# A hybrid decoder layer on one core: 32-row transposes in sample attention, one page-table transfer, ScalarE ahead of VectorE at shared PSUM banks, and larger convolution transposes

## The chip, the cores and the metric

The kernel runs on one core of one Trainium2 chip. The core has five engines with instruction streams of their own: TensorE (PE in the profile, its weight loads PEld), VectorE (DVE), ScalarE (ACT), GpSimd (POOL) and SyncE (SP, which here only issues transfers). TensorE writes to PSUM, eight banks of 128 partitions by 512 float32 values; the other engines copy from there to SBUF. The metric is the device time of one execution in microseconds. The kernel before takes 2293.38 us (median of three runs, 2289.61 to 2296.15).

## The reference

One step of a one-layer decoder trunk, all in float32: 256 prompt tokens and 8 sample sequences of 8 tokens, model width 2048. Cut to what matters here:

```
mod = silu(c) @ w_ada + b_ada                      # shift, scale, gate
h = rms_norm(x) * (1 + scale) + shift
a_qkv, a_z, a_b, a_a, b_q, b_k, b_v, b_z, i_q, i_k, i_w, g_a, g_b = split(h @ w_in)
# mixer A: short convolution (width 4, with a state of 3 old inputs), gated delta rule
qkv, conv_new = causal_short_conv(a_qkv, state_conv, conv_w)
y_a, s_new = gated_delta_rule(q, k, v, g, beta, state_gdn) -> norm, * silu(z)
# mixer B: an indexer picks the 256 best keys of each query, then attention over them
logits = einsum('bqhd,bkd->bqhk', i_q, kidx); score = sum_h relu(logits) * i_w
idx = top_k(score, 256)
y_b = softmax(q k_sel^T) v_sel * silu(b_z)
# for the samples, keys come from paged caches: kidx = cache_kidx[page_table], K, V likewise
out = x + gate * rms_norm((sigmoid(g_a) * (y_a @ w_pa) + sigmoid(g_b) * (y_b @ w_pb)) @ w_out)
```

Each sample has 1024 cached keys in 8 pages of 128. The outputs include the new delta-rule state and the last three inputs of the convolution (`conv_new`) for the prompt and for each sample.

## The kernel before

**The stream.** After a startup (`startup`, about 146 us, in which `w_ada` and the first blocks of `w_in` are read), TensorE goes through 480 units (`stream`, L342). A unit multiplies half of the 2048 rows of one 128-column block of weights with the 320 tokens: 24 matmuls of 128x320, since float32 is built from a high and a low part of weight and input (`whi`, `wlo`; `xh`, `xl`). ScalarE writes `whi` and VectorE `wlo` from the raw block, two units ahead (`split_ahead`, L326). The results go to two PSUM banks, `pm`. The order of the units is fixed: queries of the indexer, of attention, the gate of attention and gate A (units 0 to 127), then the delta-rule inputs in eight groups of two query/key heads and four value heads (units 128 to about 351; the profile calls its stage 780 to 1810 us), then gate B, the output projections and `w_out`.

**Side work.** Everything else is written as Python generators, and the order of the program is the order in which they are called: after the 12th and the 24th matmul of a unit, `side_round` (L259) lets each generator go on whose `yield` time has come by a clock of the kernel's own (`class Clock`, L68, which prices each instruction when the program is built). What a generator emits there stands on each engine's queue in that order, and every engine runs its queue in order. A generator that needs a PSUM bank takes it from the ring `ps_side` of six banks (`need`, `psum`), and gives it back when it has emitted the last reader; banks go round in turn.

**Sample attention** is one generator (`sample_branch`, L1125 on). For each of the eight samples, `keys_t` turns 8 blocks of 128x128 indexer keys (two banks of four, copied by VectorE); then come the scores (`qiS`, `wsel`), 32 rounds of top-k on VectorE, and per sample: `k_trans` (16 blocks of keys in four banks, copied by ScalarE and VectorE in turn), the products with the queries (`qS`, `esel`), the softmax, the transposes of the probabilities (8 blocks and one of 64 columns), the product with V (the last part from `vS`) and the output transpose. A transpose is a matmul with an identity matrix: the block is the loaded operand, and `ident` moves through. The keys are gathered by indices that `rows` (L753) computes from the page table, which `fetch` (L748) reads in eight transfers, each to 16 partitions.

**Convolution.** For each group, `conv_gen` (L674 on) brings old inputs (24 rows) and taps (4 rows) of 8 blocks of 128 channels to a tile `cst` of [28, 512], turns four blocks at a time (28x128 each), and VectorE copies them to `cs`. When a group's inputs are done, `ct_gen` (L1475) turns four blocks of 128x27 (`ct`) into a PSUM bank, ScalarE copies 27x512 to `cst`, and SP sends two or four transfers to the outputs.

**Delta-rule chains.** For each of 16 heads, `prompt_chain` (L1770) runs a chain of steps, each of which multiplies into one bank that both ScalarE and VectorE then read. In step 1 (names `w`, `wf`) ScalarE and VectorE take turns per value head: ScalarE scales the first 128 columns, VectorE scales the same columns, then both the next 128. Step 3 (`x1`, `ot`) and step 4 take turns likewise; `sample_chain` step 2, `bz_done` and `out_done` have VectorE first. In the program, two such readers of one bank wait for each other.

## Time and profile before

| What | Value |
|---|---|
| Median of three runs | 2293.38 us (2289.61 to 2296.15) |
| The profiled execution: its own time; its span in the trace | 2290.62 us; 2288.9 us |
| PE (matmuls) busy | 2207.7 us, 96% of the span |
| PEld (weight loads) busy | 2072.5 us, 91% |
| DVE, ACT, POOL busy | 1368.2 (60%), 1012.9 (44%), 470.6 us (21%) |
| 3 x 3328 stream matmuls of 128x320 on `w_in` | 1063.8, 1031.1 and 1029.5 us busy |
| Bytes read, written from HBM | 382.10 MB, 47.89 MB |

How to read it: every instruction is emitted through a helper, so all have line L56, and rows are told apart by the names of their tiles. `ps<-ident,a` is a transpose into a side bank of a block from the buffers `a` (keys, probabilities), `pm<-xh,whi` a stream matmul. Matmuls overlap: a row's length counts the run of one matmul through the array, so costs on TensorE are read from the starts of successive rows. Time after `[` is idle time before an instruction, with what ended it. The execution's own time is 1.7 us longer than the span.

### The profile page before, as it was taken

How to read it: one execution, taken by the hardware profiler on the slowest of the kernel's cores; microseconds unless marked ns; L12 is line 12 of the kernel's file. 1: busy time of each engine (PE TensorE's matmuls, PEld its weight loads, DVE VectorE, ACT ScalarE, POOL GpSimd, SP SyncE). 2: the span in 40 equal slices, each digit the busy share in tenths (PEclk: the TensorE clock that was granted, in tenths of full speed). 3: DMA queues.
4: the chain of work that ended last, by engine and by line, in shares of the span. 5: the costliest groups of instructions: out<-in, count | busy, mean ns of one | idle time of the engine just before them, and what ended most of it. 6: DMA issues, size and time to landing. Idle time of an engine off the chain costs nothing.

```text
span 2288.9 us, 41315 instructions
## 1 busy us (share of the span) xinstructions
PE 2207.7 (96%) x16448; PEld 2072.5 (91%) x16448; DVE 1368.2 (60%) x2666; ACT 1012.9 (44%) x2191; POOL 470.6 (21%) x624
## 2 busy tenths in 40 slices
PE   5989999999999999999999999999999999999997
PEld 3778988999988999898989898989898999999997
DVE  3333445889744567676868686868655545555433
ACT  2224355433333355554746464646454533333342
POOL 2000010000000026080818081818080000000000
PEclk9999999999999999999999999999999999999999
DMA  9989544334465557465757575756575866544543
GB/s 301 345 279 289 168 159 142 111 111 147 161 214 193 187 170 220 141 209 154 234 151 221 157 229 147 222 155 217 163 225 156 276 222 196 186 153 148 166 138 102
DMA packets 472961, 432.96 MB, mean 189 GB/s; under 512 B 63736, under 2 KB 461704, under 8 KB 470400
## 3 DMA queue, kind: packets, MB, share of 16 engines
q1 hardware_dynamic: 468384, 406.61, 57.0%
q0 software_dynamic: 3840, 21.02, 2.6%
q8 instruction: 129, 2.11, 0.4%
q10 hardware_dynamic: 544, 2.70, 0.4%
q14 instruction: 64, 0.52, 0.1%
HBM read 382.10 MB, written 47.89 MB: 188 GB/s over the span
## 4 chain that ended last, share of the span: by engine, by line
PE 77%; DVE 10%; ACT 4%; DMA 4%; POOL 2%; issue 1%; SPq 1%; DVEq 0%; POOLq 0%; ACTq 0%
PE pm L56 63%; PE ps L56 14%; DVE S L56 2%; DVE wlo L56 2%; DMA raw<-in_w_ada_dram 2%; SPq L56 1%; ACT whi L56 1%; DVE ps L56 1%; POOL X L56 1%; POOL tmpx L56 1%; ACT ot L56 1%; DVE w L56 1%; ACT ps L56 1%; DVE st L56 1%; DMA raw<-in_w_in_dram 0%
## 5 line engine op out<-in xcount | busy, mean ns | idle before, releaser
L56 PE MATMUL pm<-xh,whi 128*128 128x320 f32 x3328 | 1063.8, 320 | 2.4 <-ACT whi L56 2.4
L56 PE MATMUL pm<-xh,wlo 128*128 128x320 f32 x3328 | 1031.1, 310 | 5.8 <-DVE wlo L56 5.7
L56 PE MATMUL pm<-xl,whi 128*128 128x320 f32 x3328 | 1029.5, 309 | 0.0
L56 DVE TENSOR_TENSOR wlo<-raw,whi 128x1024 fp32r<-128x1024 f32 x480 | 600.6, 1255 | 377.4 <-ACT whi L56 376.4
L56 PEld LDWEIGHTS pm<-xh,whi 128*128 128x128 f32 x3328 | 627.2, 188 | 33.4 <-issue 25.4
L56 PEld LDWEIGHTS pm<-xh,wlo 128*128 128x128 f32 x3328 | 626.3, 188 | 8.7 <-DVE wlo L56 8.5
L56 PEld LDWEIGHTS pm<-xl,whi 128*128 128x128 f32 x3328 | 627.1, 188 | 1.0
L56 ACT ACTIVATE whi<-raw 128x1024 fp32r<-128x1024 f32 x480 | 504.4, 1056 | 262.4 <-PE pm L56 223.9
L56 POOL TENSOR_TENSOR X<-X,tmpx 48x31 f32<-48x31 f32 (+15 forms) x248 | 182.9, 738 | 19.4
L56 POOL TENSOR_TENSOR tmpx<-blk,X 48x31 f32<-48x31 f32 (+15 forms) x248 | 170.4, 687 | 44.2 <-DMA blk<-d_b 25.8
L56 PE MATMUL pm<-y1h,wlo 128*128 128x320 f32 x512 | 157.9, 308 | 0.7 <-DVE wlo L56 0.7
L56 PE MATMUL pm<-y1h,whi 128*128 128x320 f32 x512 | 157.8, 308 | 0.0
L56 PE MATMUL pm<-y1l,whi 128*128 128x320 f32 x512 | 157.8, 308 | 0.0
L56 POOL TENSOR_TENSOR sc<-sc,mh 128x6 f32<-128x6 f32 (+1 forms) x24 | 42.3, 1764 | 450.1 <-DVE sc L56 436.4
L56 DVE SCALAR_TENSOR_TENSOR ps<-xp,cs,ps 128x344 f32<-128x344 f32 x192 | 111.5, 581 | 6.8
L56 POOL TENSOR_TENSOR rfin<-rfin,mh 128x3 f32<-128x3 f32 x1 | 0.8, 848 | 495.5 <-DVE rfin L56 495.5
L56 PEld LDWEIGHTS pm<-y1h,wlo 128*128 128x128 f32 x512 | 95.9, 187 | 0.9 <-DVE wlo L56 0.9
L56 PEld LDWEIGHTS pm<-y1l,whi 128*128 128x128 f32 x512 | 96.0, 187 | 0.0
L56 PEld LDWEIGHTS pm<-y1h,whi 128*128 128x128 f32 x512 | 96.0, 187 | 0.0
L56 ACT ACTIVATE vt<-ps,sc 128x128 f32<-128x128 f32 (+1 forms) x112 | 42.5, 410 | 81.2 <-DVE w L56 64.1
L56 DVE SCALAR_TENSOR_TENSOR S<-S,gtr,ps 128x128 f32<-128x128 f32 x256 | 67.5, 343 | 1.2 <-PE ps L56 1.1
L56 ACT ACTIVATE xp<-pm 128x256 f32<-128x256 f32 (+1 forms) x128 | 31.9, 302 | 71.9 <-PE pm L56 71.7
(310 smaller groups left out, 2322.1 us busy)
## 6 DMA issues: line engine op xcount, KB each, us to landing
raw<-in_w_in_dram SPq DMA_DIRECT2D x176, 1024.0 KB
raw<-in_w_pa_dram SPq DMA_DIRECT2D x32, 1024.0 KB
rawx<-in_w_ada_dram SPq DMA_DIRECT2D x17, 1024.0 KB
a<-in_w_ada_dram SPq DMA_DIRECT2D x16, 1024.0 KB
S<-in_state_gdn_dram SPq DMA_DIRECT2D x32, 512.0 KB
out_dram<-S SPq DMA_DIRECT2D x32, 512.0 KB
raw<-in_w_pb_dram SPq DMA_DIRECT2D x16, 1024.0 KB
raw<-in_w_out_dram SPq DMA_DIRECT2D x16, 1024.0 KB
```

The source lines that it names most:

```text
L56: made = fn(*args, **kw)
```

## The change

Four things are changed.

- **Sample attention's transposes.** `tr4` splits a 128x128 transpose in four of 32 rows, each on its own 32 rows of the array and into its own bank; `out4` copies each bank, with a stride, to its place: ScalarE the even banks, VectorE the odd ones. `keys_t`, `k_trans` and the transposes of the probabilities use it. A step asks for four (or five) side banks at once where it asked for one, several times.
- **Page table.** One transfer to 8 partitions, one of 16 rows each, into a tile that VectorE has zeroed; a matmul with the matrix `samer` then spreads it to all partitions.
- **ScalarE first** where ScalarE and VectorE read one bank: `bz_done`, `prompt_chain` steps 1, 3 and 4, `sample_chain` step 2 and `out_done`. `Clock` now lets a reader of a bank start after the other engine's readers of it, and prices a 32-row transpose at 0.01.
- **Convolution.** `cst` becomes two tiles of [128, 256] that hold two channel ranges at rows 0 to 27 and 64 to 91, so that two transposes of 92x128 do what four of 28x128 did (eight input transfers a group, as before). `ct` is [128, 4, 32], zeroed at the start; one transpose of 128x128 takes the place of four of 128x27, ScalarE copies 128x128, and SP sends eight transfers for each of a group's two calls instead of four or two.

```diff
@@ class Clock @@
-                return max(outs[0].shape[-1], 32) * 2 / 2400.0
+                return 0.01 if ins[0].shape[0] == 32 else max(outs[0].shape[-1], 32) * 2 / 2400.0
...
+        if name in ("vector", "scalar"):
+            banks = {a.tensor.name for a in outs + ins if a.space == MEM.PSUM}
+            for b in banks:
+                start = max([start] + [t for e, t in self.bank.get(b, {}).items() if e != name])
@@ helpers @@
+    def tr4(self, banks, j, in_):
+        for g in range(4):
+            r = slice(32 * g, 32 * g + 32)
...
+            self.nc.tensor.transpose(banks[g][:, 32 * j:32 * j + 32], in_[r], self.ident[r, r])
+    def out4(self, banks, n, dst):
+        d = dst.rearrange("p (j g c) -> p j g c", g=4, c=32)
+        for g, p in enumerate(banks):
+            v = p[:, 0:32 * n].rearrange("p (j c) -> p j c", c=32)
+            if g % 2:
+                self.nc.vector.tensor_copy(d[:, :, g, :], v)
+            else:
+                self.act(d[:, :, g, :], v)
+            self.ps_side.put(p)
@@ conv_gen @@
-            for k in range(4):
-                self.tr(p[:, 28 * k:28 * k + 28], t[0:28, 128 * k:128 * (k + 1)])
+            for k in range(2):
+                self.tr(p[:, 128 * k:128 * k + 92], t[0:92, 128 * k:128 * (k + 1)])
@@ attn_consts: fetch, rows @@
-            for s in range(PAGES):
-                nc.gpsimd.dma_start(pt[16 * s:16 * s + 16, :],
-                                    i["page_table"][:, s:s + 1].rearrange("b o -> o b").to_broadcast([16, NB]))
+            nc.gpsimd.dma_start(pt.rearrange("(s r) b -> s r b", r=16)[:, 0, :], i["page_table"].rearrange("b s -> s b"))
...
-            nc.vector.tensor_scalar(ptf, pt, page, 16.0, op0=OP.subtract, op1=OP.mult)
+            nc.vector.tensor_copy(ptf, pt)
+            p = self.ps_main.get()
+            self.mm(p[:, 0:NB], self.samer, ptf)
+            self.ts(ptf, p[:, 0:NB], page, 16.0, OP.subtract, OP.mult)
@@ k_trans (keys_t and the probabilities alike) @@
-            for s in range(4):
-                yield from self.need(self.ps_side)
...
-                for e in range(4):
-                    self.tr(p[:, 128 * e:128 * e + 128], k[:, 128 * e:128 * e + 128])
...
+            yield from self.need(self.ps_side, 4)
+            ps = [self.psum() for _ in range(4)]
+            for j in range(16):
+                self.tr4(ps, j, K[b][:, 128 * j:128 * j + 128])
+            self.out4(ps, 16, K[b])
@@ ct_gen @@
-        for e in range(4):
-            self.tr(p[0:27, 128 * e:128 * e + 128], ct[:, e, :])
-        self.act(s, p[0:27, :])
+        self.tr(p[:, 0:128], ct.rearrange("p e r -> p (e r)"))
+        self.act(st[:, 0:128], p[:, 0:128])
...
+        for e, c0 in enumerate(cols):
+            nc.sync.dma_start(cp[:, c0:c0 + 128], st[32 * e:32 * e + 3, 0:128])
+            nc.sync.dma_start(cs[:, c0:c0 + 128], st[32 * e + 3:32 * e + 27, 0:128])
@@ prompt_chain step 1 (steps 3 and 4 alike) @@
         for v in range(2):
             self.act(wf[:, v, :], p[:, 128 * v:128 * v + 128], AF.Copy, scale=s(v, 0))
+        for v in range(2):
             self.ts(wt[:, v, :], p[:, 128 * v:128 * v + 128], stl(v, 0), None, OP.mult)
```

Since the clock prices have changed, the planner puts side work at other places of the stream. Three places follow, each first before and then after the change.

The first is TensorE's queue in the score phase of sample attention (units 45 to 46), where `a_...,qiS` are a sample's logits, `a_...,wsel` their weighted sum, and `pm` the stream. Before:

```order
L56 MATMUL ps_69<-a_1087,qiS 128x512
L56 MATMUL ps_70<-a_1087,qiS 128x512
L56 MATMUL ps_71<-kidxT,qiS 128x64
L56 MATMUL pm_66<-xh,whi_80 128x320
L56 MATMUL pm_66<-xl,whi_80 128x320
L56 MATMUL pm_66<-xh,wlo_83 128x320
```

After, a place near unit 46:

```order
L56 MATMUL ps_71<-ident,a_1086 128x32
L56 MATMUL ps_72<-a_1087,wsel 8x512 x2
L56 MATMUL ps_72<-a_1087,wsel 8x64
L56 MATMUL ps_68<-a_1086,qiS 128x512
L56 MATMUL ps_67<-a_1086,qiS 128x512
L56 MATMUL ps_69<-kidxT,qiS 128x64
L56 MATMUL ps_70<-a_1087,wsel 8x512 x2
L56 MATMUL ps_70<-a_1087,wsel 8x64
L56 LDWEIGHTS ident_b
L56 MATMUL ps_71<-bp,ident_b 128x128
```

Before, a sample's logits stand between stream matmuls, and its two `wsel` rows come 12 stream matmuls later; after, the last transposes, the weighted sums of two samples, the logits of the last and the first `ident_b` products of the next part stand in one row with no stream matmul among them.

The second is TensorE's queue at the end of sample attention, the last sample's product with V (`a,a` and `vS`). Before, in unit 121, with the output transpose `ps_72<-ident,a_1089` 23 rows further down, in unit 122:

```order
L56 MATMUL pm_66<-xh,wlo_82 128x320
L56 MATMUL ps_71<-a_1085,a_1088 64x128 x16
L56 MATMUL ps_71<-vS,a_1088 64x128 x2
L56 MATMUL pm_66<-xh,whi_79 128x320
L56 MATMUL pm_66<-xl,whi_79 128x320
L56 MATMUL pm_66<-xh,wlo_82 128x320
```

After, just ahead of unit 128, which opens the delta-rule stage:

```order
L56 MATMUL pm_66<-xl,whi_79 128x320
L56 MATMUL pm_66<-xh,wlo_82 128x320
L56 MATMUL ps_68<-a_1084,a_1087 64x128 x16
L56 MATMUL ps_68<-vS,a_1087 64x128 x2
L56 MATMUL ps_67<-ident,a_1088 128x128
L56 MATMUL pm_65<-xh,whi_80 128x320
```

The last product with V and the last output transpose moved from units 121 and 122 to the end of unit 127, behind one another, with no stream matmul between them.

The third is VectorE's queue around steps 1 and 4 of a prompt chain in the delta-rule stage, with the engines whose signals a row waits for; `w` is the result of VectorE's scaling, and ScalarE reads the same bank `ps` (for its `vt` in step 1, its `ot` in step 4). Before:

```order
L56 SCALAR_TENSOR_TENSOR S_6349<-S_6349,gtr,ps_71 128x128 x3
L56 TENSOR_TENSOR wlo_82<-raw_76,whi_79 128x1024 [waits DMAHW1_49,Activation_49]
L56 TENSOR_SCALAR w_6340<-ps_72,sc_6351 128x128 [waits DVE_49,Activation_49]
L56 TENSOR_SCALAR w_6340<-ps_72,sc_6351 128x128 [waits Activation_49]
L56 TENSOR_SCALAR w_6345<-ps_69,sc_6351 128x128 [waits PE_49]
L56 TENSOR_SCALAR w_6345<-ps_69,sc_6351 128x128
```

After:

```order
L56 SCALAR_TENSOR_TENSOR S_7148<-S_7148,gtr,ps_72 128x128 [waits PE_49]
L56 SCALAR_TENSOR_TENSOR S_7148<-S_7148,gtr,ps_72 128x128 x3
L56 TENSOR_SCALAR w_7139<-ps_68,sc_7150 128x128 [waits Activation_49]
L56 TENSOR_SCALAR w_7139<-ps_68,sc_7150 128x128 [waits DVE_49]
L56 TENSOR_SCALAR w_7144<-ps_70,sc_7150 128x128 [waits Activation_49]
L56 TENSOR_SCALAR w_7144<-ps_70,sc_7150 128x128
```

Before, the two rows of step 1 (`w_6340`) wait one after the other for ScalarE, which takes its second half only after VectorE's first, and the rows of step 4 (`w_6345`) wait for TensorE alone; after, both steps' rows (`w_7139`, `w_7144`) stand behind all of ScalarE's readings of their bank.

## Rows read from the trace of the kernel before

**Rows 1.** The page, the chain that ended last, by engine.

```profile
PE 77%; DVE 10%; ACT 4%; DMA 4%; POOL 2%; issue 1%; SPq 1%; DVEq 0%; POOLq 0%; ACTq 0%
```

**Rows 2.** Windows by stage: engines' busy us (xcount), TensorE clock, DMA share, GB/s.

```profile
0.00:180.00 180.00, 140.91 (x1138) 106.67 (x1139) 59.03 (x153) 48.24 (x84) 14.69 (x29) 0.94 0.95 299
...
600.00:780.00 180.00, 180.00 (x1380) 156.17 (x1380) 85.75 (x154) 63.59 (x120) 16.35 (x25) 1.00 0.58 195
780.00:1810.00 1030.00, 1006.52 (x7828) 961.17 (x7828) 726.18 (x1639) 550.65 (x1399) 425.27 (x552) 1.00 0.63 190
```

**Rows 3.** Timeline, PE, 16 transposes of one sample's keys (start, us, what).

```profile
604.22 1.91 PE L56 MATMUL ps<-ident,a 128*128 128x128 f32 x16
...
606.11 0.31 PE L56 MATMUL pm<-xl,whi 128*128 128x320 f32 x1
```

**Rows 4.** Timeline, PE, 16 transposes and then four of convolution inputs.

```profile
612.74 1.91 PE L56 MATMUL ps<-ident,a 128*128 128x128 f32 x16
614.58 0.43 PE L56 MATMUL ps<-ident,cst 28*128 28x28 f32 x4
...
615.19 0.31 PE L56 MATMUL pm<-xl,whi 128*128 128x320 f32 x1
```

**Rows 5.** Timeline, PE, the last three of these four.

```profile
614.66 0.34 PE L56 MATMUL ps<-ident,cst 28*128 28x28 f32 x3
```

**Rows 6.** Groups by form, PE (xcount | busy us, mean ns | idle before).

```profile
L56 PE MATMUL ps<-ident,cst 28*128 28x28 f32 x64 | 6.8, 224 | 0.0
```

**Rows 7.** Timeline, PE, first four matmuls on four groups of 32 rows.

```profile
938.28 0.50 PE L56 MATMUL ps<-w,ktok 32*128 32x256 f32 x4
```

**Rows 8.** Timeline, PE, the first of these alone.

```profile
938.28 0.48 PE L56 MATMUL ps<-w,ktok 32*128 32x256 f32 x1
```

**Rows 9.** Timeline, PE, all 16 of these and what surrounds them.

```profile
937.33 1.02 PE L56 MATMUL ps<-w,kq 128*128 128x256 f32 x4
938.28 1.15 PE L56 MATMUL ps<-w,ktok 32*128 32x256 f32 x16
...
939.61 0.31 PE L56 MATMUL pm<-xl,whi 128*128 128x320 f32 x1
```

**Rows 10.** Timeline, PE, four transposes of convolution outputs.

```profile
1139.01 0.60 PE L56 MATMUL ps<-ident,ct 128*27 128x128 f32 x4
...
1139.59 0.31 PE L56 MATMUL pm<-xl,whi 128*128 128x320 f32 x1
```

**Rows 11.** Tile cst, issues on SP's queue (ns min/median/max, first and last start).

```profile
L56 SPq DMA_DIRECT2D out_dram<-cst x48: 257/302/1997, 820.0 to 1683.9; - x48
```

**Rows 12.** Tile pt, its page-table transfers (columns as above).

```profile
L56 POOL DMA_DIRECT2D pt<-in_page_table_dram x8: 528/531/1467, 21.9 to 27.9; - x8
```

**Rows 13.** Chain of waits, 60 to 140 us (start, us, what).

```profile
112.43 11.60 DMA raw<-in_w_ada_dram
```

**Rows 14.** Waits, 780 to 1810 us (total us, times, longest).

```profile
ACT vt L56 <- DVE w L56: 64.1, 32, 5.2
...
PE ps L56 <- ACT w L56: 12.2, 7, 2.2
...
PE pm L56 <- DVE wlo L56: 5.0, 5, 2.1
```

**Rows 15.** Timeline, all engines, one prompt chain's wait.

```profile
1184.02 1.81 DVE L56 SCALAR_TENSOR_TENSOR ps<-xp,cs,ps 128x344 f32<-128x344 f32 x3
...
1186.12 0.37 ACT L56 ACTIVATE vt<-ps,sc 128x128 f32<-128x128 f32 x1 [4.10 <-DVE w L56]
...
1186.81 0.92 PE L56 MATMUL ps<-w,kq 128*128 128x256 f32 x3 [2.17 <-ACT w L56]
```

**Rows 16.** Timeline, all engines, evacuations of transposed keys.

```profile
614.28 1.08 ACT L56 ACTIVATE a<-ps 128x512 f32<-128x512 f32 x2
...
615.56 1.28 DVE L56 COPY a<-ps 128x512 f32<-128x512 f32 x2
```

**Rows 17.** Tile vS, second part of each product with V (four a sample).

```profile
L56 PE MATMUL ps<-vS,a x32: 269/294/320, 623.3 to 757.7; 64*64 64x128 f32 x32
```

More of the change, by code (lines that the diff above doesn't have):

```diff
@@ L73, in __init__ @@
         self.t = dict.fromkeys(("tensor", "vector", "scalar", "gpsimd", "sync", "dma"), 0.0)
-        self.written, self.used = {}, {}
+        self.written, self.used, self.bank = {}, {}, {}
         self.last = 0.0
@@ L172, in enter @@
             end += 0.2 if name == "tensor" else 0.1
+        if name in ("vector", "scalar"):
+            for b in banks:
+                self.bank.setdefault(b, {})[name] = end
         by = "dma" if "dma" in op else name
@@ L398, in build @@
         self.csr = Ring([c.tile([128, 8, 28], F32, name=f"cs{j}") for j in range(2)])
-        self.cst = Ring([c.tile([28, 512], F32, name="cst")])
+        self.cst = Ring([c.tile([128, 256], F32, name=f"cst{j}") for j in range(2)])
+        for t in self.cst.free:
+            self.nc.gpsimd.memset(t, 0.0)
         self.CS, self.CSV = {}, {}
@@ L681, in conv_gen @@
         cw = i["conv_w"][0]
-        for part, cols in enumerate((((256 * g, 256), (2048 + 256 * g, 256)), ((4096 + 512 * g, 512), ))):
+        for part, cols in enumerate(((256 * g, 2048 + 256 * g), (4096 + 512 * g, 4352 + 512 * g))):
             yield from self.need(self.cst)
@@ L1141, in keys_t @@
             raw = raws[b]
-            for half in range(2):
-                yield from self.need(self.ps_side)
-                p = self.psum()
-                for s in range(4):
-                    k = 4 * half + s
-                    self.tr(p[:, 128 * s:128 * s + 128], raw[:, 128 * k:128 * k + 128])
-                nc.vector.tensor_copy(raw[:, 1024 + 512 * half:1536 + 512 * half], p)
-                self.ps_side.put(p)
+            yield from self.need(self.ps_side, 4)
+            ps = [self.psum() for _ in range(4)]
+            for k in range(8):
+                self.tr4(ps, k, raw[:, 128 * k:128 * k + 128])
+            self.out4(ps, 8, raw[:, 1024:2048])
         while self.iq_n < 12:
@@ L1221, in k_trans @@
         def k_trans(b):
-            for s in range(4):
-                yield from self.need(self.ps_side)
-                p = self.psum()
-                k = K[b][:, 512 * s:512 * s + 512]
-                for e in range(4):
-                    self.tr(p[:, 128 * e:128 * e + 128], k[:, 128 * e:128 * e + 128])
-                if s % 2:
-                    nc.vector.tensor_copy(k, p)
-                else:
-                    self.act(k, p)
-                self.ps_side.put(p)
+            yield from self.need(self.ps_side, 4)
+            ps = [self.psum() for _ in range(4)]
+            for j in range(16):
+                self.tr4(ps, j, K[b][:, 128 * j:128 * j + 128])
+            self.out4(ps, 16, K[b])
         yield from load(K, ck, 0)
@@ L1349, in gdn_open @@
         self.XT = Ring([b.tile([128, 12, 128], F32, name=f"XT{j}") for j in range(1)])
-        self.ct = Ring([a.tile([128, 4, 27], F32, name=f"ct{j}") for j in range(2)])
+        self.ct = Ring([a.tile([128, 4, 32], F32, name=f"ct{j}") for j in range(2)])
+        for t in self.ct.free:
+            nc.gpsimd.memset(t, 0.0)
         self.mask3 = a.tile([128, 384], F32, name="mask3")
@@ L1368, in gdn_open @@
             nc.gpsimd.memset(t, 0.0)
-        self.gdna = [(self.csr, 2), (self.cst, 1)]
+        self.gdna = [(self.csr, 2), (self.cst, 2)]
         self.gdna += [(r, len(r.free)) for r in (self.xp, self.cu, self.cth, self.R, self.vf,
@@ L1807, in prompt_chain @@
         for v in range(2):
-            hc = hv + v
-            self.stt(x1[:, v, :], p[:, 128 * v:128 * v + 128], self.neG[:, 1, hc:hc + 1], vt[:, 1, v, :], OP.mult, OP.add)
-            self.act(ot[:, 1, v, :], p[:, 256 + 128 * v:384 + 128 * v], AF.Copy, scale=self.eG[:, 1, hc:hc + 1])
+            self.act(ot[:, 1, v, :], p[:, 256 + 128 * v:384 + 128 * v], AF.Copy, scale=self.eG[:, 1, hv + v:hv + v + 1])
+        for v in range(2):
+            self.stt(x1[:, v, :], p[:, 128 * v:128 * v + 128], self.neG[:, 1, hv + v:hv + v + 1], vt[:, 1, v, :],
+                     OP.mult, OP.add)
         self.ps_side.put(p)
@@ L1818, in prompt_chain @@
             self.act(x1[:, v, :], p[:, 128 * v:128 * v + 128], AF.Copy, scale=s(v, 1))
+        for v in range(2):
             self.ts(wt[:, v, :], p[:, 128 * v:128 * v + 128], stl(v, 1), None, OP.mult)
```

58 lines of the change are left out of this document (27 added, 31 removed).

## Prediction

> **What bounds the kernel now.** I read the chain that ended last first: 77% of it lies on PE [rows 1]. The windows by stage say where PE is free. It is full in the stage of sample attention (180.00 of 180 us) and busy 1006.52 of 1030 us in the delta-rule stage, so some 23 us there are waits; at the start it is idle 39 of 180 us, with the DMA engines at 0.95 [rows 2]. Outside the start I therefore price the change in two ways only: what it takes off or adds to PE's queue, and whether PE's waits grow or shrink. Work of VectorE, ScalarE or SP costs nothing until PE waits for it. The granted clock is 1.00 in both later stages, so nothing is to be won there.
>
> The sum is made against the profiled execution: span 2288.9 us, its own time 2290.6. That is 2.8 us under the median of the runs, 2293.4; at the end I add these 2.8 us.
>
> **Part by part.**
>
> *Keys and probabilities.* The 16 transposes of a sample's keys start at 604.22 and the second stream matmul behind them at 606.11; less one stream step of 0.147 that is 1.75 us, or 0.109 each [rows 3]. Eight indexer blocks so cost 0.88, nine of probabilities 0.98. What four 32-row transposes cost in place of one has no row. The nearest are the convolution's 28-row transposes: from 612.74 to 615.19 stand 16 of 128 rows, four of 28 and one stream step, so four of 28 cost 2.45 - 0.147 - 1.75 = 0.56 us [rows 3, 4]. They are 0.06 apart, since three take 0.34 and one alone 0.224 [rows 5, 6]; four steps are 0.25, and 0.31 are left, which I read as the price of going into the shape of few rows and out again. Whether four of them on four row groups run beside each other is seen in the matmuls on `ktok`: the first four fill 0.50 us together and the first alone 0.48 [rows 7, 8], so four start within 0.02 us; 16 of them cost 939.61 - 938.28 - 0.147 = 1.18 us, 0.07 each, where the full-height ones of as many columns take about 0.24 each (four from 937.33 to 938.28) [rows 9]. So groups overlap, loads included, and I price four 32-row transposes as one 28-row one, 0.062 us. Keys are then 8 x 0.062 + 0.31 = 0.81 instead of 0.88, `k_trans` 16 x 0.062 + 0.31 = 1.30 instead of 1.75, probabilities 0.50 + 0.11 + 0.31 = 0.92 instead of 0.98. Over eight samples that is 8 x 0.58 = 4.7 us less. Bounds: if only the starts count, and four follow one another at the pace of the first four (three gaps in 0.02 us, 0.007 each), a block takes 0.03, and the 32 blocks of a sample save another 32 x 0.034 = 1.1 us, 13 us in all; if the four run one after another at 0.062, a block takes 0.25 and a sample 32 x 0.186 = 6.0 us more, 43 us in all.
>
> Two rules of the Trainium skill speak against the change here, both on its page "TensorE: Matmul & The Clock Gate". The section "LDWEIGHTS (loading the stationary operand)" says that a load of 32x128 takes as long as one of 128x128, since only the columns count; if the four loads did not overlap, the sum would be that of the +43 bound, and the 16 matmuls at 0.07 us, loads included, speak for an overlap [rows 9]. The section "Wait — 56ns, not 53.3ns?" of the Trainium skill's page says that matmuls never start closer than about 25 ns however few their columns; four starts within 0.02 us do not agree with it where the row groups differ [rows 7, 8]. By that rule four transposes would be an estimated 0.10 us, and the whole sum about 0 instead of what follows.
>
> *Convolution inputs.* 16 times, four transposes at 0.56 us [rows 4] become two of 92 rows, which I price like full-height ones without a change of shape, 0.16 to 0.22: 16 x 0.38 = 6.1 us less. *Convolution outputs.* Four cost 1139.59 - 1139.01 - 0.147 = 0.43 us [rows 10]; one costs 0.109 [rows 3]. 16 x 0.32 = 5.2 us less. Both lie on PE's queue, so I count all of it, 11.3 us. (0 at the least if PE then waits in the same stage for what paces it there; that is a rival below.) ScalarE's copy of `ct` shrinks, VectorE's stays. SP issues 10 transfers more per group, 80 in all at about 0.30 us [rows 11], and 24 us over a stage of 1030 us on a queue that only issues; the weights come two units ahead. I take 0; if one raw block is late because of eight issues ahead of it (2.4 us), it costs a wait of at most that, per group 2.4, in all 19 at the far end.
>
> *Page table.* Seven transfers fewer on POOL at 0.53 us [rows 12]; `rows` gets one copy and one matmul more. It stands before the point where the chain waits 11.60 us for `w_ada` [rows 13]. Taken as 0; uncovered, a copy and a matmul are under 1 us.
>
> *ScalarE first.* PE waits 12.2 us in 7 waits for ScalarE's `w` [rows 14]. One of them, read: ScalarE's second `vt` waits 4.10 us for VectorE's `w`, which stands behind three convolution steps of 1.81 us together, and PE's next product starts 2.17 us late [rows 15]. After the change ScalarE reads both halves at once and does not need VectorE; but that product also takes VectorE's `w`, which still stands behind those steps. So the chain of three handovers becomes one, and ScalarE's second reading (0.37) is out of the way by then. I take half, 6 us, between 0 and 12.2. In turn VectorE, in order, now waits for ScalarE in step 4 too, where ahead of it was TensorE only, and behind it stands `wlo`. PE waits for `wlo` 5.0 us in 5 waits [rows 14]; I add 3 us, between 0 and 24 (a rival). Net -3.
>
> *Places in the stream.* Four or five of six banks must now be free at once, and banks are freed after ScalarE and VectorE have copied: two copies of 128x512 take 1.08 and 1.28 us [rows 16], both engines work beside each other, and PE is covered by the half unit of stream, 12 x 0.147 = 1.76 us. Where there is no stream between, the cover is gone. The order shows two such places. At unit 46 four steps of the score phase stand in one lump; each is fed by an evacuation, about 0.6 us with its handover, twice or so uncovered per step: 3 us. At unit 128 the last product with V and the last output stand right ahead of the delta-rule stage: 2 us. For the five-bank step of the probabilities, eight times 0.3 us, 2 to 3 us. Together +8, between 0 (the planner found the banks free) and 20 (each of 8 samples and both lumps at 1 us per uncovered copy, twice).
>
> **The sum.** -4.7 - 11.3 - 3 + 8 = -11 us: 2290.6 becomes 2279.6, and with the 2.8 us to the median 2282.4. I write 2282.5. The own range of this case is 2275 to 2290.
>
> **Rivals.**
> - *Given back.* What PE saves is waited for later. The last sample's product with V comes at 757.7 now [rows 17], well ahead of the delta-rule stage at about 781; after the change it stands right before it, so a sample's chain (the 32 products are 134.4 us from first to last, 19.2 a sample) has no stream of its own to hide under. If half of the last one is bare, 10 us come back: 2292. For it: the compressed order. Against: stream matmuls still stand between all steps but the last.
> - *Issue bound.* Four small transposes cost as much as the one that they replace, 0.109 [rows 3], and the shape costs 0.31 at each of 24 sites: +7.4 instead of -4.7, 2294.5. Against it are the starts within 0.02 us [rows 7, 8]; for it, that no row has such short loads and matmuls in turn at that density. (The Trainium skill's floor of 25 ns, in the page and section above, is such a mechanism.)
> - *Row groups one after another.* +43 instead of -4.7: 2330. Against it: 16 matmuls at 0.07 us [rows 9].
> - *VectorE held by ScalarE* (slower than before). In each of 16 chains VectorE's `w` rows stand behind ScalarE, which has `whi` or the gate's work ahead of it; the next `wlo` is late and PE with it. Price: at 1.5 us a chain (waits for `wlo` are up to 2.1 us [rows 14]) 24 us instead of the net -3: 2309. From 0.5 us a chain on it makes up for all the rest (16 x 0.5 = 8, the forecast's 11 without its own 3), and from 0.9 on the time is above 2300. For it: DVE is busy 726 us of 1030 [rows 2] with little slack in bursts. Against it: ScalarE, at 551 us, is the freer one, and ScalarE itself now never waits there.
> - *More than that.* Only issue counts for transposes (-13), all 12.2 us come back, and the banks are never short: -13 - 11.3 - 12.2 + 3 is about -33, 2260.
>
> **Chances.** Forecast 0.48; given back 0.16; issue bound 0.08; one after another 0.06; VectorE held 0.12; more 0.10. What a measurement here can tell from no change is about 0.3%, 6.9 us: below 2286.5 is faster, above 2300.3 slower. Of the forecast's own range four fifths lie below 2286.5, so faster is 0.39 + 0.10 and a little of the two middle cases, 0.52; slower is 0.06 + 0.11, 0.17; the rest, 0.31, is the same. The range runs from 2264, which cuts half of the last case, to 2300, which leaves out the two slow ones.
>
> **What would show it.** Right: the `cst` and `ct` transposes take about 0.2 and 0.11 us from the stream where they stand, `k_trans` about 1.3 us, starts of four transposes within 62 ns; PE's waits for ScalarE's `w` at about half; the delta-rule stage shorter by 12 to 17 us; attention by 5 at most. Wrong: a block of four transposes at 0.1 us or more; waits of PE for `wlo` that grow by over 10 us; idle PE ahead of unit 128 or at unit 46 of more than 8 us; weights late behind SP's issues.

## The result, and the profile after

The changed kernel takes 2260.61 us (median, 2257.41 to 2261.71), the kernel before 2293.44 in the same comparison: a ratio of 0.9856 (95% interval 0.9838 to 0.9873), 33 us less. The forecast was 2282.5 with a range down to 2264: the direction was right, the size a third of what came. Its profiled execution takes 2261.71 us, with a span of 2260.0.

The stream gives a ruler. It has 11520 matmuls of 128x320, 24 a unit, so the start of each 24th is the start of a unit. Durations in us from unit to unit in the profiled executions (one execution each; over the profiles of this study the startup with the old page table takes 143.8 to 148.4 us, and the delta-rule stage in the order of before takes 1026.2 us here and 1032.5 in e11, whose time is that of before, so single differences of a few us mean little):

| Units | What | before | after | ScalarE first alone |
|---|---|---|---|---|
| up to 0 | startup | 146.8 | 141.9 | 148.1 |
| 0 to 32 | queries of the indexer | 156.5 | 156.5 | 155.3 |
| 32 to 96 | scores, top-k, prompt attention | 295.6 | 290.5 | 291.9 |
| 96 to 128 | sample attention | 182.1 | 178.4 | 182.4 |
| 128 to 352 | delta rule | 1026.2 | 1011.2 | 1002.2 |
| 352 to 479 | tail | 463.0 | 463.3 | 462.8 |

The chain that ended last, by engine, after ([rows 1] before). PE has 3 points less, and POOL (the inverses of the delta rule) 4 more.

```profile
PE 74%; DVE 8%; POOL 6%; DMA 5%; ACT 3%; SPq 2%; issue 2%; DVEq 0%; POOLq 0%; ACTq 0%
```

The transposes came out as priced. `k_trans` of one sample, on PE (start, us, what), answers to [rows 3]:

```profile
658.49 1.19 PE L56 MATMUL ps<-ident,a 32*128 32x32 f32 x64
...
659.86 0.31 PE L56 MATMUL pm<-xl,whi 128*128 128x320 f32 x1
```

From 658.49 to the second stream matmul are 1.37 us; with the step of 0.147 off, and 0.09 added by which the first transpose starts later than a stream matmul would (658.25 + 0.147), it is 1.32 us, where 1.30 was forecast and 1.75 stood before. Keys so cost 0.82 (0.81 forecast), probabilities 0.85 (0.92). Four 32-row transposes are about 0.063 us apart: the row groups do run beside each other. In the groups by form (xcount | busy us, mean ns), which answer to [rows 6], the convolution's transposes are

```profile
L56 PE MATMUL ps<-ident,cst 92*128 92x92 f32 x32 | 5.2, 242 | 0.0
...
L56 PE MATMUL ps<-ident,ct 128*128 128x128 f32 x16 | 4.4, 272 | 0.0
```

and a pair of 92 rows takes 0.19 us out of the stream, one of 128x128 0.11; both as priced.

What did not come out is seen in the waits of the delta-rule stage (total us, times, longest), which answer to [rows 14]:

```profile
POOL tmpx L56 <- DMA blk<-d_b: 100.7, 4, 26.1
...
ACT whi L56 <- DMA raw<-in_w_in_dram: 73.5, 21, 8.8
...
PE pm L56 <- DVE wlo L56: 11.0, 14, 1.6
```

ScalarE's 64.1 us of waits for VectorE's `w` at `vt`, and TensorE's 12.2 us for ScalarE's `w`, have no row any more. In their place ScalarE waits 73.5 us for raw weights (10.3 before), POOL 100.7 for `blk` in the inverses (25.8 before), and TensorE 11.0 for `wlo` (5.0 before). In the stage's own 767.3 to 1778.5 us TensorE's waits for `wlo` are 14.2, since one of 3.9 stands ahead of the window; it comes back below.

### The profile page after: what moved, and what is told of

Read it like the earlier page. It is cut to its first block, busy times and chain, and to the rows that moved or that the text cites. A ratio compares the mean times of both kernels' runs of the same rounds, so it can differ in the third digit from the quotient of the medians.

```text
span 2260.0 us, 42925 instructions
## 1 busy us (share of the span) xinstructions
PE 2186.4 (97%) x17138; PEld 2052.5 (91%) x17138; DVE 1352.0 (60%) x2668; ACT 1017.0 (45%) x2223; POOL 458.8 (20%) x621
## 4 chain that ended last, share of the span: by engine, by line
PE 74%; DVE 8%; POOL 6%; DMA 5%; ACT 3%; SPq 2%; issue 2%; DVEq 0%; POOLq 0%; ACTq 0%
PE pm L56 61%; PE ps L56 14%; POOL X L56 3%; POOL tmpx L56 3%; DVE wlo L56 2%; SPq L56 2%; DVE S L56 1%; DVE ps L56 1%; ACT ot L56 1%; DMA raw<-in_w_in_dram 1%; DMA blk<-d_b 1%; DVE BT L56 1%; ACT whi L56 1%; DMA raw<-in_w_ada_dram 1%; DMA rawx<-in_w_ada_dram 1%
## 5 line engine op out<-in xcount | busy, mean ns | idle before, releaser
L56 PE MATMUL pm<-xh,wlo 128*128 128x320 f32 x3328 | 1031.6, 310 | 14.3 <-DVE wlo L56 14.2
L56 POOL TENSOR_TENSOR tmpx<-blk,X 48x31 f32<-48x31 f32 (+15 forms) x248 | 172.6, 696 | 119.5 <-DMA blk<-d_b 100.7
L56 ACT ACTIVATE a<-ps 128x256 f32<-128x256 f32 (+3 forms) x96 | 50.1, 558 | 36.6 <-PE ps L56 34.0
```

The source lines that it names most:

```text
L56: made = fn(*args, **kw)
```

## The experiments

All ratios are to the kernel before on the same chip, with 95% intervals.

| Kernel | us | ratio |
|---|---|---|
| e1 page table alone | 2291.1 | 0.9988 (0.9977 to 0.9999) |
| e2 convolution alone | 2289.6 | 0.9968 (0.9958 to 0.9978) |
| e3 32-row transposes alone | 2293.3 | 0.9993 (0.9983 to 1.0002) |
| e4 ScalarE first alone | 2264.7 | 0.9868 (0.9852 to 0.9884) |
| e5 changed kernel without convolution part | 2259.7 | 0.9848 (0.9832 to 0.9865) |
| e6 before, output transfers cut in 16 | 2302.6 | 1.0035 (1.0022 to 1.0048) |
| e7 ScalarE first in step 1 | 2293.4 | 0.9995 (0.9986 to 1.0005) |
| e8 changed kernel, planner without shared banks | 2258.4 | 0.9838 (0.9821 to 0.9854) |
| e9 ScalarE first in step 4 | 2289.7 | 0.9981 (0.9969 to 0.9993) |
| e10 ScalarE first in step 3 | 2287.7 | 0.9971 (0.9958 to 0.9983) |
| e11 as e6, order of before | 2295.0 | 1.0002 (0.9992 to 1.0011) |
| e12 e5 and e8 together | 2251.9 | 0.9809 (0.9792 to 0.9826) |
| e13 convolution alone, order of before | 2288.6 | 0.9976 (0.9962 to 0.9990) |
| e14 ScalarE first in step 4 and sample step 2 | 2269.9 | 0.9895 (0.9879 to 0.9912) |
| e15 VectorE first, grouped, steps 1, 3, 4 | 2294.5 | 1.0000 (0.9990 to 1.0010) |
| e16 e12 with the convolution part, order of e12 | 2255.4 | 0.9818 (0.9793 to 0.9842) |
| e17 e12 with the new input transposes, order of e12 | 2248.6 | 0.9799 (0.9783 to 0.9816) |
| e18 e12, output transfers cut in 16, order of e12 | 2253.1 | 0.9818 (0.9802 to 0.9835) |

**Each part alone.** The edits of e1 to e4 are those of the diff above, each by itself.

> The kernel before with the page table in one transfer and nothing else. In the profile after, the stream starts 4.9 us earlier (141.9 instead of 146.8 us), which the prediction had at 0. Theory A, the page table does it (seven transfers fewer before the startup's weights): stream start at about 142, time about 4.9 us shorter, 2288. Theory B, it is the spread of the startup's transfers from run to run: stream start anywhere between 140 and 148, also in kernels that leave the page table alone, and the time unchanged within a few us.

> The kernel before with the convolution's transposes, input tiles and output transfers changed, nothing else. Theory A, all of it lies on TensorE's queue: 14 x 0.36 + 16 x 0.32 = 10 us less in the delta-rule stage and 0.7 us in attention, 2282.5 in all. Theory B, the delta-rule stage is paced by something else (VectorE's low parts, POOL's inverses): waits of TensorE grow by about what is saved, 2288 to 2293.

> The kernel before with the 32-row transposes on four row groups (and their price in the planner), nothing else; the planner does not know that two engines exclude each other at a bank. Theory A: transposes give 5.0 us, the places of the stream cost about 3 (lumps at units 46 and 128), so 2 us less, 2291. Theory B, the new places themselves save waits of prompt attention (6.5 us less of them between units 32 and 96 in the profile after): 2284.

> The kernel before with ScalarE ahead of VectorE at the shared banks (gate of attention, chain steps, output), nothing else; the planner's prices are the old ones. Theory A, the order of readers alone gives what the profile after shows: waits of TensorE for the chains down by 16 us, waits for wlo up by 11, 5 us less in the delta-rule stage, and 5 to 6 us less of waits in prompt attention (the gate's reading of its bank): 2283. Theory B, the gain needs the planner that knows of the exclusion: waits as before, 2290 to 2294.

*e1.* The page table does it (theory A, with 2.8 us of its 4.9 in the time). With the old one the stream starts at 143.8 to 148.4 us (twelve profiles, this study's), with the new one at 140.8 to 143.9 (eight). The windows show the place (the last columns are TensorE's clock, DMA share and GB/s); before, and with the page table alone:

```profile
20.00:40.00 20.00, 10.23 (x84) 4.26 (x75) 6.09 (x9) 2.68 (x4) 7.30 (x9) 1.00 0.90 283
```

```profile
20.00:40.00 20.00, 13.89 (x87) 7.52 (x88) 8.79 (x17) 4.02 (x7) 2.32 (x2) 1.00 1.10 346
```

While the eight transfers of 16 times 8 single values are under way, the DMA engines move 283 GB/s instead of 346 (260 to 283 in the twelve profiles, 346 in each of the eight). That is 63 GB/s x 20 us = 1.3 MB less, 3.6 us at the full rate, in a stage that waits for these bytes.

*e4.* Of the parts alone, ScalarE first is nearly everything: 30 us, far past theory A (2283), and theory B is out. TensorE, VectorE and ScalarE have the same order as before in it but for the pairs turned round. 24 us lie in the delta-rule stage, 3.7 in units 64 to 96, the attention gate (`bz_done`). TensorE's idle time in the stage was 23.5 us (1026.2 less 1002.72 busy) and is 7.7 now. That is 15.8 less, while the stage is 24.0 shorter: the idle time that the profile puts before an instruction is less than what a wait costs. Before, and with ScalarE first:

```profile
781.00:1807.20 1026.20, 1002.72 (x7803) 957.37 (x7802) 725.08 (x1636) 549.32 (x1396) 425.27 (x552) 1.00 0.63 190
```

```profile
777.60:1779.80 1002.20, 994.47 (x7801) 953.80 (x7801) 720.23 (x1636) 547.09 (x1396) 424.42 (x552) 1.00 0.65 195
```

*e3.* 1.6 us, within noise, as theory A has it. In the profile the score phase (units 32 to 48) is 1.7 us longer, the rest of attention 4.7 shorter, and units 128 to 132, the first of the delta-rule stage, are 1.5 longer: the places cost some 3 us here.

*e2.* 7 us of the 10.4 priced, nearer to theory B; where the rest goes is the last question below.

**Where ScalarE first gains.** e7, e9 and e10 turn one step of the prompt chain round, e14 two banks; e15 groups the readings but leaves VectorE ahead:

```diff
# e9: step 4 (e7: step 1 likewise; e10: step 3, ot ahead of x1)
         for v in range(2):
             self.act(x1[:, v, :], p[:, 128 * v:128 * v + 128], AF.Copy, scale=s(v, 1))
+        for v in range(2):
             self.ts(wt[:, v, :], p[:, 128 * v:128 * v + 128], stl(v, 1), None, OP.mult)
# e14: e9, and in sample_chain
+        self.act(ot[:, 2], p[:, 0:256].rearrange("p (v d) -> p v d", v=2))
         for v in range(2):
             self.ts(wt[:, v, :], p[:, 128 * v:128 * v + 128], stl(v, 2), None, OP.mult)
-        self.act(ot[:, 2], p[:, 0:256].rearrange("p (v d) -> p v d", v=2))
# e15: steps 1, 3 and 4, the two loops of e9 exchanged
```

> The kernel before with ScalarE first in step 1 of the prompt chains only. ScalarE waited 64.1 us for VectorE's w rows, most of it in step 1 and step 3's like, and the whole reorder is worth 30.7 us. Theory A, step 1, whose bank stands behind VectorE's convolution steps, carries most of it: 15 to 22 us, 2273 to 2280. Theory B, the gain is spread over steps 1, 3 and 4, of the chain about a third each: 6 to 10 us, 2285 to 2289.

> The kernel before with ScalarE first only in step 4 of the prompt chains (the scaling of x1, whose bank VectorE reads for w). With step 1 turned round, ScalarE's 32 waits for VectorE's w fell to 16, but from 64.1 only to 57.9 us: the long ones are step 4's, about 3.6 us each. Theory A, these waits hold up TensorE and the weights behind them in ScalarE's queue, and step 4 carries most of the 30.7 us: 15 to 25 us, 2269 to 2279. Theory B, the gain needs several steps turned round together: under 7 us, 2287 to 2294.

> The kernel before with ScalarE first only in step 3 of the prompt chains (ot ahead of x1). ScalarE waits 33.5 us in 32 waits for VectorE's vt there. Theory A, the gain is in proportion to the waits that go: about a third of the whole, 8 to 12 us, 2282 to 2286. Theory B, these waits of about 1 us each are covered by the half unit of stream behind them (1.76 us): 0 to 3 us, 2291 to 2294.

> The kernel before with ScalarE first in step 4 of the prompt chain and in step 2 of the sample chain, nothing else. With step 4 alone, TensorE's 12.2 us of waits for ScalarE's w went, but 10.1 us of waits for ScalarE's ot came up, and ScalarE's waits for VectorE's w at ot rose from 8.2 to 31.2 us: the wait moved on to the next shared bank in ScalarE's queue, that of the sample chain's step 2. Theory A, a chain of banks behind one backlog of VectorE: with both turned round the wait is gone, 13 to 20 us, 2275 to 2282. Theory B, the parts add up singly, and most is elsewhere: 5 to 8 us, 2287 to 2290.

> The kernel before with the readings of each engine grouped in steps 1, 3 and 4 of the prompt chain, but VectorE's pair ahead of ScalarE's. There is no handover back and forth either, only who is first differs from the changed kernel. Theory A, ScalarE must not wait for VectorE's backlog (the convolution steps ahead of its reading): no gain, 0 to 4 us, 2291 to 2295, ScalarE's waits for VectorE at vt stay near 60 us. Theory B, it is the three handovers at a bank that cost: half or more of the gain, 10 to 20 us, 2275 to 2285.

Neither theory of e7 held: step 1 gains nothing that can be told. Step 4 alone gives 4.4 us (theory B), step 3 6.7 (between its two). The waits of e9 in the delta-rule stage say why so little:

```profile
ACT ot L56 <- DVE w L56: 31.2, 16, 3.8
...
PE ps L56 <- ACT ot L56: 10.1, 6, 2.2
...
ACT vt L56 <- DVE w L56: 6.9, 16, 0.6
```

The 64.1 us at `vt` [rows 14] are 6.9, and TensorE's 12.2 us for ScalarE's `w` are gone; but ScalarE now waits 31.2 us (8.2 before) at the next bank in its queue that VectorE reads first, that of the sample chain's step 2, and TensorE 10.1 us (2.1 before) for what ScalarE makes there. With that bank turned round too (e14) this is left:

```profile
ACT vt L56 <- DVE w L56: 9.5, 16, 1.7
...
PE ps L56 <- ACT ot L56: 3.6, 5, 0.7
...
PE ps L56 <- DVE w L56: 0.2, 1, 0.2
```

and the time is 24 us shorter, though step 4 alone gave 4. So a wait that moves on, as theory A has it, by more than it said. TensorE's order is the same in before, e9 and e14, so its starts can be compared one by one. In the delta-rule stage e9 gains 14.1 us at the product `ps<-w,kq` and loses 10.9 at two products that wait for ScalarE's `ot` (`ps<-w,ktok`, `ps<-vt,XT`); e14 keeps the 14.1, all but 1.0 of that loss is gone, and 6.3 more are gained at stream matmuls. Step 2 of the sample chain was not run alone: at those two products there was little for it to gain by itself (TensorE waited 2.1 us for `ot` before), but some of the 6.3 may be its own. With VectorE first but grouped (e15) nothing is gained, and ScalarE's waits are longer than before:

```profile
ACT vt L56 <- DVE w L56: 77.1, 27, 6.4
...
PE ps L56 <- ACT w L56: 16.4, 7, 2.8
```

Theory A: grouping the readings is not what gains; ScalarE must not stand behind VectorE's backlog, the convolution steps of [rows 15]. (e15 leaves the sample chain's bank as it was. The same three steps together with ScalarE first, and nothing else, were not run.)

**What the convolution part and the planner are worth.** e6 and e11 cut the output transfers of the kernel before; e11, e13, e16, e17 and e18 give the planner the old prices, so that everything else keeps its order on TensorE, VectorE and ScalarE:

```diff
# e6
-        for c0, s0, s1 in cols:
+        for c0, s0, s1 in [(c + 128 * e, a + 128 * e, a + 128 * e + 128) for c, a, b in cols for e in range((b - a) // 128)]:
# e11 (e18 likewise): the same transfers, the planner told of the old ones
-            nc.sync.dma_start(cp[:, c0:c0 + s1 - s0], s[0:3, s0:s1])
-            nc.sync.dma_start(cs[:, c0:c0 + s1 - s0], s[3:27, s0:s1])
+            for d in range(0, s1 - s0, 128):
+                for dst, r0, r1 in ((cp, 0, 3), (cs, 3, 27)):
+                    nc.sync.engine.dma_start(dst[:, c0 + d:c0 + d + 128], s[r0:r1, s0 + d:s0 + d + 128])
...
# e8 (and e12, e16 to e18): the lines of class Clock on banks taken out
# e13, e16: instructions of the new part, the planner told of the old ones
+            nc.tensor.engine.transpose(p[:, 128 * k:128 * k + 92], t[0:92, 128 * k:128 * (k + 1)], self.ident[:92, :92])
...
+            enter("tensor", "transpose", (p[:, 28 * k:28 * k + 28], f[0:28, 128 * k:128 * (k + 1)], self.ident[:28, :28]), {})
```

> The changed kernel with the convolution part taken back (four transposes each, tiles and transfers as before). In the runs so far, the convolution part alone saves 6 us of 10 to 11 priced, and ScalarE's waits for raw weights in the delta-rule stage rise from 10 to 60 us; with ScalarE first and convolution together that stage takes 1011 us, with ScalarE first alone 1002. Theory A, the convolution part gives back all it saves once the chains no longer wait, through later weights: 2252 to 2260, not slower than the changed kernel. Theory B, its 10 us are a gain here too: 2266 to 2271.

> The kernel before with each group's six output transfers of the convolution state cut into 16, as in the changed kernel (80 more issues on SP's queue, of 24 or 3 rows by 128 columns); transposes and all else as before. Theory A, the transfers are what delays the weights: ScalarE's waits for raw weights in the delta-rule stage go from 10 us towards 60, the stage is 4 to 12 us longer: 2299 to 2306. Theory B, they are free, and the places in the stream are the cause: waits stay near 10 us and the time at 2295.

> The changed kernel with a planner that does not know that ScalarE and VectorE exclude each other at a bank (all instructions the same, other places). Theory A, the reader order does the work and the planner's knowledge adds little: 2258 to 2264. Theory B, places chosen with the exclusion save waits: 5 us or more longer, 2266 to 2275. Sum of the parts run alone (page table -4.2, convolution -5.8, transposes -2.1, ScalarE first -30.7 = -42.8) would be 2252.6; if the planner's knowledge costs time, this run is nearer to that.

> The kernel before with each group's six convolution output transfers cut into 16, but priced by the planner as six, so that TensorE, VectorE and ScalarE keep the order of before word for word; only SP's queue is longer by 80 issues. With the planner's price for 16 the time was 8.4 us longer. Theory A, the issues themselves delay what stands behind them on SP: 4 us or more longer, 2298 to 2303. Theory B, the longer time came from the places that the planner chose: within 2 us of before, 2292 to 2296.

> The changed kernel without the convolution part and without the planner's knowledge of shared banks (page table, 32-row transposes and ScalarE first are left). Each was worth nothing or a loss when taken back alone (2259.7 and 2258.4 against 2260.6). Theory A, both cost by their places and add up: 2255 to 2258. Theory B, the places are chance, and the two cannot be added: 2258 to 2264. The parts measured alone (page table -4.2, transposes -2.1, ScalarE first -30.7) would give 2257.

> The kernel before with the convolution part alone, but every instruction and transfer of it priced by the planner as the old one, so that all other work keeps its place and order on every engine. With the planner's own prices this part saved 5.8 us of 10.4 priced. Theory A, the missing 4.6 us are the cost of the places that the planner chose anew: 10 us saved, 2284 to 2286. Theory B, they are lost to the transfers (more and shorter ones) or to waits that any order has: 4 to 7 us saved, 2288 to 2291.

> The changed kernel without the planner's knowledge of shared banks and with the convolution part priced as the old one (page table, 32-row transposes, ScalarE first and the new convolution transposes are all in it; the order is that of the kernel without the convolution part, 2251.9 us). Theory A, the convolution part is worth its 10 us where it moves nothing: 2240 to 2244. Theory B, with ScalarE first in place the time that it frees on TensorE is waited for elsewhere: 2248 to 2252.

> The kernel of 2251.9 us (page table, 32-row transposes, ScalarE first) with the new transposes of the convolution's inputs alone (two of 92 rows), priced by the planner as the old ones, so that all else keeps its order; the outputs' transposes and their six transfers a group stay as before. The input transposes are worth 5.8 us on TensorE's queue. Theory A, what loses time in the combined kernel (2255.4) is the output side with its 16 short transfers a group, and the input side is a gain: 2245 to 2248. Theory B, any time taken off TensorE's queue in the delta-rule stage is waited for there: 2250 to 2254.

> The kernel of 2251.9 us with its six convolution output transfers a group cut into 16 and nothing else; the planner prices six, so the order is the same on TensorE, VectorE and ScalarE. On the kernel before, the same cut cost nothing (2295.0 against 2294.9). Theory A, with ScalarE first the slack that hid the transfers is gone, and they hold back what stands behind them on SP: 5 to 12 us longer, 2257 to 2264. Theory B, they are hidden here too: 2250 to 2254.

*e6 and e11.* 80 more issues cost 8 us when the planner sees them, and nothing when it does not: the places it chooses anew cost, not the queue. (e6 has the time of its theory A, but ScalarE's waits for raw weights are 20.0 us, nearer to the 10 of B than to the 60 of A.) My reading after e2, that the loss comes of SP's longer queue, falls.

*e5, e8, e12.* The changed kernel without the convolution part takes as long as with it. The planner's knowledge of shared banks gains nothing that can be told either (e8). Without both the kernel takes 2251.9 us, and its interval lies below that of the changed kernel. The delta-rule stage takes 1011.6 us in e5, 1009.7 in e8 and 1001.9 in e12, and 1004.1 with the convolution part in e12's order (e16). e5 and e12 have the same instructions and their intervals lie apart, so between them the places that the planner chooses are the cause; 4.4 us lie in units 128 to 132 (21.0 and 16.6 us, 14.6 before), which come back below. e8 and e16 have the same instructions too, but their intervals overlap: that the convolution part loses by its places is not shown. Theory A of e5 and e8, and of e12 by more than it said; whether the two costs add up cannot be told (2 and 4 us singly, 11 together by the ratios, each to within some 5).

*e13.* In the same order, too, half of the 10 us is missing (theory B, 5.5 us). Set beside before start by start, the new transposes save 9.7 us at their own places, and TensorE loses 6.6 at others: 2.4 at one product of the inverses (`ps<-X,blk`, unit 263), where the profile names nothing that it waits for, and 2.9 at unit 189. There it arrives early and waits 3.79 us (0.94 before), on PE:

```profile
1028.88 0.31 PE L68 MATMUL pm<-xh,wlo 128*128 128x320 f32 x1
1032.98 0.41 PE L68 MATMUL pm<-xh,whi 128*128 128x320 f32 x1 [3.79 <-ACT whi L68]
```

On ScalarE `whi` stands behind a copy into `cst` (one tile, as before; the changed kernel has two). I read its wait as one for the outputs to leave that tile, though the row names another releaser, since the row of before names them; e13, and before:

```profile
1029.24 0.28 ACT L1515 ACTIVATE cst<-ps 128x128 f32<-128x128 f32 x1 [8.65 <-PE pm L68]
...
1031.88 1.05 ACT L68 ACTIVATE whi<-raw 128x1024 fp32r<-128x1024 f32 x1
```

```profile
1029.90 0.59 ACT L56 ACTIVATE cst<-ps 27x512 f32<-27x512 f32 x1 [6.23 <-DMA out_dram<-cst]
```

And on SP those outputs stand behind `d_x<-blk`, which waits for POOL's inverse; e13, and before:

```profile
1024.42 0.31 SPq L68 DMA_DIRECT2D d_x<-blk  x1
1024.84 0.27 SPq L1528 DMA_DIRECT2D out_dram<-cst  x1
...
1027.82 0.30 SPq L1529 DMA_DIRECT2D out_dram<-cst  x1
```

```profile
1026.82 0.31 SPq L56 DMA_DIRECT2D d_x<-blk  x1
1027.23 0.67 SPq L56 DMA_DIRECT2D out_dram<-cst  x2
```

POOL is done 2.4 us earlier than before, and eight transfers take 3.3 us where two took 0.7, so the last output leaves at 1028.1 instead of 1027.9. Unit 189 starts 1.0 us earlier than before, unit 188 3.8. At the same place e16, the same part beside ScalarE first, has the wait too, and there the row names the outputs; on ScalarE, and on PE:

```profile
1019.26 0.28 ACT L1525 ACTIVATE cst<-ps 128x128 f32<-128x128 f32 x1 [7.96 <-DMA out_dram<-cst]
```

```profile
1023.00 0.63 PE L68 MATMUL pm<-xh,whi 128*128 128x320 f32 x1 [3.10 <-ACT whi L68]
```

*e16 to e18.* Beside ScalarE first the convolution part in an unchanged order gains nothing that can be told (0.9818 against 0.9809). Neither do the transfers alone cost (e18, 0.9818), nor do the input transposes alone gain (e17, 0.9799), within these intervals. B is nearer in e16 and e18; e17 lies between its two, 0.6 us from A and 1.4 from B, and tells nothing. In e17 the input side of the diff above is new and the output side old. It is the fastest kernel of the study, 2248.6 us, not told from e12.

## Why the prediction was wrong, point by point

- **What bounds the kernel:** right on PE, wrong on the start. "Work of VectorE, ScalarE or SP costs nothing until PE waits for it" holds, but I took too little for what PE's waits give back (below).
- **Transposes, -4.7:** right. 8 x (0.06 + 0.43 + 0.13) = 5.0 by their starts. The shape's 0.31 and the 0.062 per four held. The rule of the Trainium skill that I weighed ("TensorE: Matmul & The Clock Gate", "Wait — 56ns, not 53.3ns?", no starts closer than about 25 ns) does not hold across row groups here: 64 starts lie within 1.19 - 0.22 = 0.97 us, 0.015 each.
- **Places in the stream, +8:** some 5 us net in the changed kernel, and the larger part by a wait that I had not named. The lump at unit 46 costs 2.2 us (units 32 to 48 take 1.7 more, though the keys' transposes save 0.5 there) and has one wait of 1.09; the end before unit 128 has one of 0.52:

```profile
377.44 1.51 PE L56 MATMUL ps<-a,wsel 128*8 128x512 f32 x6 [1.09 <-ACT a L56]
```

```profile
767.21 0.33 PE L56 MATMUL ps<-ident,a 128*128 128x128 f32 x1 [0.52 <-ACT a L56]
```

Behind unit 128 it costs more: units 128 to 132 take 19.8 us instead of 14.6. The transfers of sample attention's output (`d_yb<-ybuf`) now leave 0.6 to 3.5 us after unit 128 starts, where the last left 7.7 us ahead of it; VectorE's set-up of the delta-rule stage (`mask`) waits for them, 9.14 us instead of 0.10, and `wlo` stands behind it:

```profile
777.00 0.59 DVE L56 COPY mask<-mask 128x128 f32<-128x128 f32 x3 [9.14 <-DMA d_yb<-ybuf]
```

```profile
778.75 0.42 PE L56 MATMUL pm<-xh,wlo 128*128 128x320 f32 x1 [3.89 <-DVE wlo L56]
```

These four units take 16.2 to 17.0 us in the kernels with 32-row transposes whose planner does not know of shared banks. Units 48 to 128 are some 2 us shorter than the transposes and the gate of attention account for, so the five-bank step shows no loss.
- **Convolution, -11.3:** the instructions cost what I said, but it is not a gain of that size: 5.5 to 7 us alone, none beside ScalarE first. I had the rival that PE's saving is waited for, and gave it no part of the sum.
- **Page table, 0:** wrong, about -5 at the start of the stream and -2.8 (0.2 to 5.3) in the time. I counted POOL's issues and two instructions, and named the wait for `w_ada` [rows 13] as the cover. It is what the transfers lengthen: the cover was the cost.
- **ScalarE first, -3: the step that failed.** "I take half, 6 us, between 0 and 12.2", and +3 for VectorE; alone this part gives 30 us. The half rests on "that product also takes VectorE's `w`", and that is false: `ps<-w,kq` takes the tile `S1`, which ScalarE writes. At the place of [rows 15] the product no longer waits in e4, and starts ahead of VectorE's `w`:

```profile
1173.37 0.38 ACT L56 ACTIVATE w<-ps 128x256 f32<-128x256 f32 x1 [0.20 <-PE ps L56]
...
1175.04 1.81 DVE L56 SCALAR_TENSOR_TENSOR ps<-xp,cs,ps 128x344 f32<-128x344 f32 x3
...
1175.37 1.02 PE L56 MATMUL ps<-w,kq 128*128 128x256 f32 x4
...
1176.76 1.12 DVE L56 TENSOR_SCALAR w<-ps,sc 128x128 f32<-128x128 f32 x4
```

So all of the row came back, and not half. e4 keeps TensorE's order, so its starts can be set beside those of before: of the 24.0 us in the delta-rule stage 14.1 lie at `ps<-w,kq` (a wait of 2.17 there delays the start by 2.34, so 12.2 us by name are 14.1 in time), 6.5 at stream matmuls and 5.3 at the chains' other products, less 2.0 at a product of the inverses. Another 3.4 lie at the gate of attention (`ps<-ident,s`, units 64 to 96), which is in this part and had no term in the sum. The bound of 12.2 was too low, since a queue that no longer stands still shortens waits under other names as well. The +3 did not come: VectorE's waits for ScalarE moved (22.9 us for `vt` before, in e4 5.2 for `vt` and 17.4 for `ot`), but PE's for `wlo` in that stage went from 5.0 to 3.8.
- **The sum:** its errors partly cancel, 27 us too little for ScalarE first and up to 11 too much for the convolution. The sign "the delta-rule stage shorter by 12 to 17 us" came true, at 15.0, by luck: it was to be the convolution's 11.3 and 3 of ScalarE first, while ScalarE first alone gives 24.0 and 9 are lost again in the whole. The sign "attention by 5 at most" failed: units 32 to 128 are 8.8 us shorter.
- **Rivals.** "More than that" gave 2260, near the time, but by terms that did not come (transposes at 13 us, banks never short); it had 12.2 us for ScalarE first. "VectorE held by ScalarE" did not happen. "Given back" did: the parts alone sum to 2.8 + 7.3 + 1.6 + 30.3 = 42 us (from the ratios), the change gives 33. In part it was where I put it, 5.2 us at the start of the delta-rule stage of the 10 that I priced, though by VectorE's set-up and not by bare products (1.5 of it is in e3 too); the rest is not told apart.
- **Open:** why the freed time of the convolution part is all waited for beside ScalarE first. In e16 the new transposes save 9.2 us at their own places, set beside e12 start by start, and TensorE loses 11.4 at others: 3.9 at unit 189, by the wait for the one tile `cst` shown above; 2.7 at one kind of product of the inverses (`ps<-X,blk`), of which 1.8 are a wait that the profile names nothing for; the rest in small pieces. (In the changed kernel, with two tiles, TensorE has no wait for `whi` there.) That POOL's inverses set the pace is not shown: their waits for `blk` are 100.9 us in e8 and 30.2 in e16, the same instructions, and the two times cannot be told apart. No run took the inverses away, and sending the 16 transfers as fewer was not run.

## What to carry to other kernels

Where two engines read one bank in turn, ask which of them stands behind a backlog, and let the other read first, at every such bank on its way: here ScalarE first (busy 549 us of the stage, VectorE 725) gained 30 us, VectorE first nothing, and turning one bank round moved the wait to the next. Before taking half of a wait, check in the kernel which engine writes what the waiting instruction takes. The row that names a wait is not a bound for what a freed engine gives: all of that row came back, and as much again under other names. When work moves to the end of a stage, look for what the next stage's first instructions wait for. And what a wait hides is only hidden if it does not use what is waited for.

## What was not expected of the hardware

64 transposes of 32 rows on four groups took 1.32 us, and four of them start within 0.01 us (first to last). Eight small transfers of single values took a fifth of the DMA rate for some 20 us (283 against 346 GB/s).
